# A mixer's 32-partition transpositions replaced by one transposition and ScalarE copies, a PSUM bank lent to side work, and new costs in the build-time scheduler

## The chip, the cores and the metric

The kernel runs on one core of a Trainium2 chip. The metric is the device time of one execution in microseconds. The profile's times are those of one profiled execution; engines are TensorE (PE, with its weight loads PEld), VectorE (DVE), ScalarE (ACT), GpSimd (POOL) and SyncE (SP), whose queue issues nearly all DMAs.

## The reference

One layer of a hybrid decoder for 320 tokens: a prompt of 256 and 8 sample sequences of 8 tokens with their own states. D is 2048, all in fp32. Two recurrent mixers read one input projection:

```
proj = x @ w_in                        # q, k, v, i, f, o of mLSTM; q, f, i, g of HGRN2; two gates
# mLSTM, 4 heads (DK 256, DV 512), stabilised matrix memory
C_new = decay * C + sum_s w_end k_s v_s^T
num   = (q k^T * d) v + w_inter * (q C);  h = num / max(|den|, exp(-m))
branch_a = LayerNorm(h) * ml_norm_g * sigmoid(o)
# HGRN2, 8 heads (DK 128, DV 256)
f = lb + (1 - lb) * sigmoid(hf);  S_t = diag(f_t) S_{t-1} + (1 - f_t) i_t^T;  o_t = S_t^T q_t
branch_b = RMSNorm(o) * hg_norm_g * silu(g)
merged = sigmoid(gate_a) * (branch_a @ w_branch_a) + sigmoid(gate_b) * (branch_b @ w_branch_b)
x1 = LayerNorm(alpha * x + merged @ w_out)
y  = LayerNorm(alpha * x1 + relu(x1 @ w_up)^2 @ w_down)
```

Outputs are y for both groups and the new states: C (4 x 256 x 512, for the prompt and for each of 8 samples), n, m and S.

## The kernel before

**The weight stream.** All weights pass through TensorE as tiles of 128 output columns over 2048 inputs, in the order of tile_list: per mLSTM head four mv, two mk, two mq and two gate tiles (ga); then per HGRN head two gate tiles, hf, hq and two hi; then sixteen o tiles, the rest of the gate tiles (gb), hg and wa in turns, wb, wo, and the FFN's up and dn. A tile is two weight units of 128 x 1024. For each unit SyncE loads the raw weights (tile wr, one of three buffers), ScalarE writes their high part (wh), VectorE the residual (wl, L497), and TensorE does 24 matmuls of 320 columns (L356: high·high, high·low, low·high for eight blocks), 48 a tile, into one PSUM bank. These are the main matmuls. Some wide spare buffers (bb, carved from others later on) serve as wh and wl too.

**Side work.** Everything else, the two mixers above all, runs beside this stream. Each piece is a generator ("chain") that yields operations with an engine and a cost; `Sched` (lines 124 to 243) simulates the five engines while the program is built and emits an operation when its modelled time has come. So the costs and constants of the scheduler don't run on the chip, they set each engine's fixed order. `run_main` emits one triple of main matmuls at a time and calls `pump`, which lets the chains emit what is ready; at most 900 modelled ns of side work go on TensorE between two triples. LAT is added where a step follows one on another engine, SAME where it follows one on the same engine, and PE_LAT is a margin that TensorE's side matmuls must have. act(), dve(), dve_t() (transpositions), pe_f() and pe_r() give costs.

**Banks.** Of eight PSUM banks three belong to the main tiles (mbank) and five to side work (sbank). When a tile is done, its chain `ev_...` reads the bank and gives it back; `take` hands the next tile the bank that is free longest.

**turn.** An mLSTM head's v (1280 elements on each of 128 partitions) and an HGRN head's i (640) must be turned from "channels on partitions" to "tokens on partitions". `turn` does that with 24 VectorE transpositions a head, each from 32 partitions to 32: sixteen at L1156, eight at L1159. VectorE transposes within squares of 32 x 32, so a piece both transposes and moves the squares to other partitions.

**Stacks and states.** `stack` writes high and low parts of the samples' keys side by side (low by VectorE, L987); TensorE transposes them against the identity (L1027 for mLSTM, L1530 for HGRN). For mLSTM's sample states (`m_states`, `m_update`, `m_store`) 64 blocks of 128 x 512 are loaded (C) into one of 14 buffers (cb: six in f, eight in rx), used by matmuls in eight groups of sixteen, updated by VectorE (L1271) and stored (Cs); only after the store has landed is the buffer free for a later block's load. All these DMAs stand on SyncE's queue with the weight loads, the gates that are spilled (gaD), copies of khl and vhl for the prompt's state (kD, vD) and the heads' outputs (hH, hL).

**h_out** normalises an HGRN head's two prompt blocks and transposes each on VectorE (L1631). **ev_o** multiplies an o tile's sigmoid with mLSTM's output and splits it into high and low parts for wa.

The names f_75, f_76 and f_77 in the rows of the order are the SBUF areas f1, f2 and f3; bank_81 to bank_88 are the PSUM banks.

Of the kernel before, what the change touches and what calls it, by code (L numbers as in the profile page):

```python
# [20 lines left out]
TOK = 320  # L21
# [101 lines left out]
LAT = 140.0  # L123
SAME = 100.0
# [19 lines left out]
class Sched:  # L144
# [24 lines left out]
    def step(self, c, now):  # L169
        if c.req is None:  # L170
            try:
                c.req = c.gen.send(c.send)
            except StopIteration:
                c.done = True
                return False
            c.send = None
        kind = c.req[0]
        if kind == "wait":
            for e in c.req[1]:
                if e.t is None:  # L180
                    return False
            c.ready = max([c.ready] + [e.t for e in c.req[1]])
            c.eng = None
        elif kind == "acq":
            pool, n = c.req[1], c.req[2]
            if len(pool.free) < n:
                return False
            pool.free.sort(key=lambda x: x[0])
            got, pool.free = pool.free[:n], pool.free[n:]
            c.ready = max([c.ready] + [x[0] for x in got])  # L190
            c.eng = None
            c.send = got[0][1] if n == 1 else [x[1] for x in got]
# [76 lines left out]
def dve_t(n):  # L269
    return 155.0 + 1.07 * n  # L270
# [43 lines left out]
class Program:  # L314
# [163 lines left out]
    def prep(self, must=False):  # L478
# [103 lines left out]
    def before(self, i, t):  # L582
# [12 lines left out]
        elif kind == "o" and h == 0:  # L595
            s.until(lambda: all(m["end"].t is not None for m in self.mh))
        elif kind == "hg" and h == 0:
            s.until(lambda: all(m["end"].t is not None for m in self.hh))
            self.carve_m()
            self.carve_b()  # L600
            B = self.Part(self.f2)
            for pool in (self.sg, self.sg, self.sr, self.ld, self.ld, self.ld):
                pool.free.append((s.t["pe"], B(320)))
        if kind in ("o", "wa", "hg", "wb"):
            s.spawn(self.fetch(kind, h), 1)
        elif kind == "mk" and h == 0 and c == 0:
            self.load_ev.t = s.t["pe"]
# [312 lines left out]
    def m_S(self, h):  # L920
# [20 lines left out]
        yield ("act", act(128), lambda: self.A(ss[64:128, 0:128], E[64:128, 384:512]))  # L941
# [203 lines left out]
    def turn(self, to, x):  # L1145

        v = self.nc.vector
        n = x.shape[1]
        for a in range(4):
            p = slice(32 * a, 32 * a + 32)  # L1150
            col = lambda y: y.rearrange("p (c a k) -> p a c k", a=4, k=32)[:, a]
            for b in range(4):
# [3 lines left out]
                yield ("dve", dve_t(64 * n), lambda: v.transpose(o, i))  # L1156
            for b in range(2):
                o, i = col(to[64 + 32 * b:96 + 32 * b, 2, :]), x[p, :, NP_ + 32 * b:NP_ + 32 * b + 32]
                yield ("dve", dve_t(32 * n), lambda: v.transpose(o, i))  # L1159
# [143 lines left out]
    def sigmoid(self, p, out, r, free=()):  # L1303
# [9 lines left out]
        yield ("act", act(TOK), lambda: self.A(r, out, AF.Ln, scale=2.0 ** -LN_SH, bias=self.ln_b))  # L1313
        yield ("act", act(TOK), lambda: self.A(r, r, AF.Exp, scale=-1.0, bias=self.exp_b))
# [3 lines left out]
    def ev_hf(self, h, c, b):  # L1318
# [5 lines left out]
        yield ("act", act(TOK), lambda: self.A(u, f, AF.Identity, scale=-1.0, bias=self.one))  # L1324
# [112 lines left out]
    def h_lag(self, b, at):  # L1437
        v = self.nc.vector
        a4 = at[:, 0:TOK].rearrange("p (b r) -> p b r", r=4)
        for d in (0, 2, 1, 3):  # L1440
# [4 lines left out]
            yield ("dve", dve(n, True), lambda: v.copy_predicated(  # L1445
# [4 lines left out]
    def h_put(self, b, at, B):  # L1450
# [3 lines left out]
        elif B >= 32:  # L1454
            for j in range(64 // B):
                for i in range(2):
                    lo, c = 64 * j + B * i, 128 * i + 64 * j
                    yield ("act", act(B, True), lambda: self.A(
# [15 lines left out]
    def h_i(self, h):  # L1474
# [12 lines left out]
        yield ("act", act(256), lambda: self.A(hi, it[64:128, 2, :]))  # L1487
        yield ("dve", dve(256), lambda: v.tensor_tensor(lo, it[64:128, 2, :], hi.bitcast(F32), ALU.subtract))
# [24 lines left out]
    def h_state(self, h):  # L1513
# [18 lines left out]
        for x in range(4):  # L1532
            r = slice(32 * x, 32 * x + 32)
            yield ("act", act(256, True), lambda: self.A(kst[r, x], b[r, 0:256].rearrange("p (g k) -> p g k", g=2)))
# [80 lines left out]
    def h_out(self, h):  # L1615
# [14 lines left out]
        for i in range(2):  # L1630
            yield ("dve", dve_t(256), lambda: v.transpose(on[:, i, :], on[:, i, :]))  # L1631
# [59 lines left out]
    def ev_o(self, j, c, b):  # L1691
# [7 lines left out]
        yield rel(self.ld, x)  # L1699
        yield from self.split(g, self.bah[:, j, :], self.bal[:, j, :])  # L1700
# [388 lines left out]
```

## Time and profile before

| | |
|---|---|
| median of 3 runs | 2305.03 us (2302.9 to 2306.02) |
| the profiled execution | 2302.73 us |
| its span, first to last instruction | 2300.8 us |
| mean granted TensorE clock | 0.999 |
| DMA traffic | 424.94 MB, 185 GB/s |

The profile's page gives busy times, the span in slices, the DMA queues, the chain that ended last, the costliest groups and the DMA issues. A group's row has line, engine, operation, the tiles written and read, the shapes, the count, then busy us and mean ns, then the idle time before its instructions and what ended it. All ScalarE operations pass through one helper and so have line L350, all weight and most side matmuls L356, all SyncE transfers L359. A table by window gives each engine's busy time and count, the granted clock, the DMA engines' mean share and the rate.

### The profile page before, as it was taken

What the parts mean: (1) busy time and instruction counts of PE and PEld (TensorE: products, weight loads), DVE (VectorE), ACT (ScalarE), POOL (GpSimd) and SP (SyncE); (2) the same over time, 40 slices, a digit from 0 to 9 for tenths busy, and PEclk for the clock granted to TensorE, in tenths of its full rate; (3) what the DMA queues carried; (4) which work ended last, traced back from release to release, by engine and by line L of the source; (5) the groups of instructions that cost most, each with busy time, mean ns of one, the idle gap of its engine ahead of it and who ended that gap; (6) DMA issues with size and microseconds to landing.
All of it is one profiled execution on the core that took longest, in us unless ns stands there. A gap on an engine that the chain in (4) does not pass through costs nothing.

```text
span 2300.8 us, 38921 instructions
## 1 busy us (share of the span) xinstructions
PE 2289.6 (100%) x15592; PEld 2246.1 (98%) x15592; DVE 1458.9 (63%) x2634; ACT 1036.6 (45%) x1653; POOL 13.5 (1%) x37
## 2 busy tenths in 40 slices
PE   9999999999999999999999999999999999999998
PEld 9999899999999999999999999999999999999998
DVE  6786786788888886555555767654444444444455
ACT  5443445455555565444433446533433343234334
POOL 0000000000000000000000000000000000000000
PEclk9999999999999999999999999999999999999999
DMA  7667977755565564555545644444444444444475
GB/s 284 211 186 259 295 250 229 259 176 185 191 207 187 166 198 167 180 174 170 176 172 175 214 163 147 147 147 149 154 147 150 152 147 153 149 147 154 149 228 193
DMA packets 214574, 424.94 MB, mean 185 GB/s; under 512 B 83572, under 2 KB 110068, under 8 KB 213368
## 3 DMA queue, kind: packets, MB, share of 16 engines
q1 hardware_dynamic: 209512, 415.97, 53.7%
q0 software_dynamic: 4736, 6.29, 1.0%
q8 instruction: 122, 2.00, 0.3%
q14 instruction: 60, 0.49, 0.1%
q10 hardware_dynamic: 144, 0.20, 0.0%
HBM read 371.48 MB, written 50.90 MB: 184 GB/s over the span
## 4 chain that ended last, share of the span: by engine, by line
PE 69%; DVE 3%; ACT 1%; issue 0%; ACTq 0%; DVEq 0%
PE bank L356 69%; DVE wl L497 1%; ACT wh L350 0%; DVE f L1156 0%; DVE f L1445 0%; ACT f L350 0%; DVE f3m L1973 0%; DVE f3m L1980 0%; ACT f3m L350 0%; DVE f L1159 0%; DVE f L1315 0%; DVE f L1316 0%; DVE f L1631 0%; DVE f L1698 0%; DVE f L1309 0%
## 5 line engine op out<-in xcount | busy, mean ns | idle before, releaser
L356 PE MATMUL bank<-xh,wh 128*128 128x320 f32 (+1 forms) x2504 | 794.6, 318 | 0.0
L356 PE MATMUL bank<-xh,wl 128*128 128x320 f32 (+1 forms) x2504 | 774.8, 310 | 0.0
L356 PE MATMUL bank<-xl,wh 128*128 128x320 f32 (+1 forms) x2504 | 772.2, 309 | 0.0
L497 DVE TENSOR_TENSOR wl<-wr,wh 128x1024 fp32r<-128x1024 f32 x440 | 538.7, 1224 | 361.4 <-ACT wh L350 358.3
L350 ACT ACTIVATE wh<-wr 128x1024 fp32r<-128x1024 f32 x440 | 465.4, 1058 | 524.7 <-PE bank L356 495.6
L356 PEld LDWEIGHTS bank<-xh,wh 128*128 128x128 f32 x2504 | 472.0, 189 | 17.2 <-issue 15.3
L356 PEld LDWEIGHTS bank<-xl,wh 128*128 128x128 f32 x2504 | 471.5, 188 | 3.3
L356 PEld LDWEIGHTS bank<-xh,wl 128*128 128x128 f32 x2504 | 471.8, 189 | 0.2 <-DVE wl L497 0.2
L497 DVE TENSOR_TENSOR bb<-wr,bb 128x1024 fp32r<-128x1024 f32 x162 | 198.5, 1225 | 193.7 <-ACT bb L350 193.5
L350 ACT ACTIVATE bb<-wr 128x1024 fp32r<-128x1024 f32 x162 | 171.6, 1059 | 294.6 <-PE bank L356 277.5
L356 PE MATMUL bank<-ra,wh 128*128 128x320 f32 x1008 | 275.9, 309 | 0.7 <-DVE ra L1672 0.7
L356 PE MATMUL bank<-ra,bb 128*128 128x320 f32 x1096 | 255.2, 309 | 0.0
L356 PE MATMUL bank<-xh,bb 128*128 128x320 f32 (+1 forms) x1136 | 253.8, 309 | 0.0
L356 PE MATMUL bank<-rxb,bb 128*128 128x320 f32 x1088 | 249.0, 309 | 0.0
L356 PEld LDWEIGHTS bank<-xh,bb 128*128 128x128 f32 x1136 | 191.0, 188 | 0.0
L356 PE MATMUL bank<-rxb,wh 128*128 128x320 f32 x608 | 187.5, 308 | 0.0
L356 PE MATMUL bank<-rxb,wl 128*128 128x320 f32 x608 | 187.5, 308 | 0.0
L356 PEld LDWEIGHTS bank<-ra,bb 128*128 128x128 f32 x1096 | 184.9, 187 | 0.0
L356 PEld LDWEIGHTS bank<-rxb,bb 128*128 128x128 f32 x1088 | 184.2, 187 | 0.0
L356 PEld LDWEIGHTS bank<-ra,wh 128*128 128x128 f32 x1008 | 180.9, 187 | 0.9 <-DVE ra L1672 0.9
L356 PE MATMUL bank<-xl,bb 128*128 128x320 f32 (+1 forms) x568 | 175.5, 309 | 0.0
L356 PE MATMUL bank<-bb,wh 128*128 128x320 f32 (+1 forms) x536 | 119.0, 313 | 0.0
(259 smaller groups left out, 2244.4 us busy)
## 6 DMA issues: line engine op xcount, KB each, us to landing
wr<-wt SPq DMA_DIRECT2D x602, 512.0 KB, 3.3
rx<-C SPq DMA_DIRECT2D x34, 256.0 KB, 5.6
Cs<-rx SPq DMA_DIRECT2D x34, 256.0 KB, 4.8
f<-C SPq DMA_DIRECT2D x30, 256.0 KB, 5.5
Cs<-f SPq DMA_DIRECT2D x30, 256.0 KB, 4.1
f<-first SPq DMA_DIRECT2D x6, 704.0 KB, 9.6
vD<-ra SPq DMA_DIRECT2D x4, 1024.0 KB, 5.2
f<-S SPq DMA_DIRECT2D x8, 512.0 KB, 5.0
```

What stands on the lines that cost most here:

```text
L350: return self.nc.scalar.activation(out, in_, func, **kw)
L356: self.nc.tensor.matmul(*a, **kw)
L497: self.V().tensor_tensor(lo, raw, hi.bitcast(F32), ALU.subtract)
```

## The change

Four things. `turn` transposes its source once, in place, on all 128 partitions (VectorE), and then moves the 24 pieces with ScalarE copies; `h_out` transposes two blocks in one instruction. One of the three main banks is lent to side work from the first mk tile to the first hg tile: two main and six side banks in between. `ev_o` waits before its split, for tiles from 7 on, for the last HGRN head's scores (j < 12) or its state (from 12 on). And the scheduler's account: LAT 140 becomes 130; SAME 100 becomes 127 for ScalarE and 113 for VectorE; a step behind TensorE adds 200 (PE_OUT) where it added LAT; transpositions cost 295 + 1.05 n where it was 155 + 1.07 n; operations on part of the partitions cost 122 more (PART); three ScalarE operations with a pointer as bias or scale count it; masked copies get four fixed costs; the weights' two preparations count as 1048 and 1034 elements.

```diff
-LAT = 140.0
-SAME = 100.0
+LAT = 130.0
+SAME = dict(act=127.0, dve=113.0)
+PE_OUT = 200.0
+PART = 122.0
...
-            if c.eng != kind or after:
+            if c.eng == "pe" and kind != "pe" and not after:
+                r += PE_OUT
+            elif c.eng != kind or after:
                 r += LAT
-            elif kind in ("act", "dve"):
-                r += SAME
+            elif kind in SAME:
+                r += SAME[kind]
...
 def dve_t(n):
-    return 155.0 + 1.07 * n
+    return 295.0 + 1.05 * n
...
-        e = s.use("act", max(at, self.raw_at[u]) + LAT, act(1024))
+        e = s.use("act", max(at, self.raw_at[u]) + LAT, act(1048))
...
-        e = s.use("dve", e + LAT, dve(1024))
+        e = s.use("dve", e + LAT, dve(1034))
...
             self.carve_b()
+            self.mbank.free.append(self.sbank.free.pop())
...
         elif kind == "mk" and h == 0 and c == 0:
+            s.until(lambda: self.mbank.free)
+            self.sbank.free.append(self.mbank.free.pop())
...
         n = x.shape[1]
+        t = yield ("dve", dve_t(TOK * n), lambda: v.transpose(x, x))
...
-                yield ("dve", dve_t(64 * n), lambda: v.transpose(o, i))
+                yield ("act", act(64 * n) + PART, lambda: self.A(o, i), (t,))
...
-                yield ("dve", dve_t(32 * n), lambda: v.transpose(o, i))
+                yield ("act", act(32 * n) + PART, lambda: self.A(o, i), (t,))
...
-            yield ("dve", dve(n, True), lambda: v.copy_predicated(
+            yield ("dve", (415.0, 385.0, 320.0, 155.0)[d], lambda: v.copy_predicated(
...
-        yield ("act", act(256), lambda: self.A(hi, it[64:128, 2, :]))
-        yield ("dve", dve(256), lambda: v.tensor_tensor(lo, it[64:128, 2, :], hi.bitcast(F32), ALU.subtract))
+        yield ("act", act(256) + PART, lambda: self.A(hi, it[64:128, 2, :]))
+        yield ("dve", dve(256) + PART, lambda: v.tensor_tensor(lo, it[64:128, 2, :], hi.bitcast(F32), ALU.subtract))
...
-        for i in range(2):
-            yield ("dve", dve_t(256), lambda: v.transpose(on[:, i, :], on[:, i, :]))
+        yield ("dve", dve_t(512), lambda: v.transpose(on[:, 0:2, :], on[:, 0:2, :]))
...
+        if j > 6:
+            yield wait(self.hh[HH - 1]["aT" if j < 12 else "sdone"])
```

The lines left out give PART to four more costs and the pointer to three ScalarE costs. The change adds lines, so in its rows L354 stands for L350, L360 for L356, L363 for L359, L501 for L497 and L994 for L987. What it moves shows in two places.

The first is VectorE in HGRN head 3, before the low part of the samples' stack (L987, then L994) that TensorE's first transposition of this head (L1530 of before) waits for. Before:

```order
L497 TENSOR_TENSOR wl<-wr,wh 128x1024
L1419 TENSOR_TENSOR f_75<-f_75 128x40
L1156 STREAM_TRANSPOSE f_76<-f_75 32x4x32
L1466 COPY_PREDICATED f_75<-lmask,bank_88 128x40x4
L1156 STREAM_TRANSPOSE f_76<-f_75 32x4x32
L1664 TENSOR_SCALAR misc<-misc 128x1
L1056 TENSOR_SCALAR misc<-misc 128x1
L1156 STREAM_TRANSPOSE f_76<-f_75 32x4x32
L987 TENSOR_TENSOR f_76<-f_75,f_76 128x16x8
```

After the change:

```order
L501 TENSOR_TENSOR wl<-wr,wh 128x1024
L1323 SCALAR_TENSOR_TENSOR f_76<-f_76 128x320
L1067 TENSOR_TENSOR misc<-misc 128x1
L1424 TENSOR_TENSOR f_75<-f_75 128x16x8
L1479 COPY_PREDICATED f_75<-lmask,bank_86 128x16x8
L994 TENSOR_TENSOR f_76<-f_75,f_76 128x16x8
```

Three pieces of turn have left the way to the stack. They stand on ScalarE, which in the same head now has:

```order
L354 ACTIVATE wh<-wr 128x1024 x2
L354 ACTIVATE f_76<-f_75 32x4x32 x4
L354 ACTIVATE f_76<-f_75 32x2x32 x2
L354 ACTIVATE f_76<-bank_88,misc 128x256
L354 ACTIVATE f_76<-f_75 32x4x32 x4
L354 ACTIVATE f_76<-f_76 128x320
L354 ACTIVATE f_76<-f_75 32x2x32
L354 ACTIVATE wh<-wr 128x1024
```

Eleven of the 24 pieces stand in a row of side work between two weight copies. The second place is SyncE's queue around the last state load for the first group of mLSTM head 2. Before, from the store that frees the last buffer (the row ahead of vD) to the load into it (the last rx<-C):

```order
L359 DMA Cs<-rx 128x512
L359 DMA vD_114<-ra 128x2048
L359 DMA wr<-wt 128x1024
L359 DMA Cs<-rx 128x512
L359 DMA rx<-C 128x512
L359 DMA Cs<-rx 128x512
L359 DMA rx<-C 128x512
L359 DMA wr<-wt 128x1024
```

After the change, from the load before it:

```order
L363 DMA rx<-C 128x512
L363 DMA Cs<-rx 128x512
L363 DMA kD_110<-ra 32x32x32
L363 DMA Cs<-rx 128x512
L363 DMA kD_110<-ra 32x32x32
L363 DMA wr<-wt 128x1024
L363 DMA hL_200<-f_76 128x4x64
L363 DMA kD_110<-ra 32x32x32
L363 DMA rx<-C 128x512 x2
L363 DMA Cs<-rx 128x512
```

The 1 MB copy vD no longer stands between the store and the load; three of the four copies kD and an output hL stand there instead.

More of the change, by code (lines that the diff above doesn't have):

```diff
@@ L940, in m_S @@
         yield ("act", act(384), lambda: self.A(sh, E[:, 0:384]))
-        yield ("act", act(128), lambda: self.A(ss[64:128, 0:128], E[64:128, 384:512]))
+        yield ("act", act(128) + PART, lambda: self.A(ss[64:128, 0:128], E[64:128, 384:512]))
         yield ("dve", dve(384), lambda: v.tensor_tensor(sl, E[:, 0:384], f(sh), ALU.subtract))
@@ L1312, in sigmoid @@
         yield ("act", act(TOK), lambda: self.A(out, out, AF.Exp))
-        yield ("act", act(TOK), lambda: self.A(r, out, AF.Ln, scale=2.0 ** -LN_SH, bias=self.ln_b))
-        yield ("act", act(TOK), lambda: self.A(r, r, AF.Exp, scale=-1.0, bias=self.exp_b))
+        yield ("act", act(TOK, False, 1), lambda: self.A(r, out, AF.Ln, scale=2.0 ** -LN_SH, bias=self.ln_b))
+        yield ("act", act(TOK, False, 1), lambda: self.A(r, r, AF.Exp, scale=-1.0, bias=self.exp_b))
         yield ("dve", dve(TOK), lambda: v.scalar_tensor_tensor(out, out, 1.0, r, ALU.add, ALU.mult))
@@ L1323, in ev_hf @@
         yield ("dve", dve(TOK, mode=2), lambda: v.tensor_scalar(f, u, l1, lb, ALU.mult, ALU.add))
-        yield ("act", act(TOK), lambda: self.A(u, f, AF.Identity, scale=-1.0, bias=self.one))
+        yield ("act", act(TOK, False, 1), lambda: self.A(u, f, AF.Identity, scale=-1.0, bias=self.one))
         yield post(m["fd"])
@@ L1457, in h_put @@
                     lo, c = 64 * j + B * i, 128 * i + 64 * j
-                    yield ("act", act(B, True), lambda: self.A(
+                    yield ("act", act(B, True) + PART, lambda: self.A(
                         at[64 * j:64 * j + B, c + B:c + 2 * B], b[lo:lo + B, c // 2:c // 2 + B]))
@@ L1533, in h_state @@
             r = slice(32 * x, 32 * x + 32)
-            yield ("act", act(256, True), lambda: self.A(kst[r, x], b[r, 0:256].rearrange("p (g k) -> p g k", g=2)))
+            yield ("act", act(256, True) + PART, lambda: self.A(kst[r, x], b[r, 0:256].rearrange("p (g k) -> p g k", g=2)))
         yield rel(self.sbank, b)
```

## Prediction

> **What bounds the kernel now.** I read the busy shares first, then the busy time by stage, then the waits of TensorE, then single places on the timeline. The page's first row, and four rows of the table by stage (window, length, then busy time and count of PE, PEld, DVE, ACT, POOL, granted clock, DMA share, GB/s):
>
> ```profile
> PE 2289.6 (100%) x15592; PEld 2246.1 (98%) x15592; DVE 1458.9 (63%) x2634; ACT 1036.6 (45%) x1653; POOL 13.5 (1%) x37
> 180.00:406.00 226.00, 225.78 (x1520) 209.27 (x1519) 172.20 (x340) 102.30 (x169) 0.00 (x0) 1.00 0.79 255
> 300.00:350.00 50.00, 50.00 (x343) 44.49 (x342) 45.37 (x96) 22.02 (x36) 0.00 (x0) 1.00 0.92 291
> 420.00:860.00 440.00, 437.37 (x3055) 426.68 (x3054) 370.89 (x961) 248.81 (x534) 4.74 (x13) 1.00 0.60 192
> 860.00:2277.00 1417.00, 1416.34 (x9648) 1415.62 (x9647) 759.07 (x999) 579.59 (x764) 5.90 (x8) 1.00 0.47 162
> ```
>
> TensorE sets the end. From 860 to 2277 us it does 9648 matmuls in 1417 us, one every 147 ns at granted clock 1.00, and that stretch keeps its order on TensorE; nothing is to be had there. A gain can only come from 93 to 860 us, where the two recurrent mixers run beside the weights. There TensorE seems full too, but a busy row hides part of a wait: a matmul is booked for 0.31 us while the next starts 0.147 us after it. VectorE is the crowded helper (172.20 of 226 us in the mLSTM stage, 370.89 of 440, 84%, in the HGRN stage); ScalarE has room (102.30 of 226, 248.81 of 440, 57%). The waits of TensorE say who is late (engine, line, waited for: us in total, times, longest):
>
> ```profile
> PE bank L1530 <- DVE f L987: 1.5, 3, 0.7
> PE bank L356 <- DVE rh L1488: 1.1, 2, 0.6
> ...
> PE bank L1212 <- DVE f L1049: 0.7, 1, 0.7
> PE bank L356 <- DVE ra L1672: 0.7, 1, 0.7
> ```
>
> The three rows on L987, L1488 and L1049 are VectorE work that the mixers need. Their six waits make 3.3 us, and each hides up to 0.16 us in the booking (0.31 − 0.147), so at most 4.3 us. The row L1672 is one wait after 860 us, where the order stays. One of the six on the timeline (start, duration, engine, line):
>
> ```profile
> 603.36 0.30 PE L356 MATMUL bank<-xh,wl 128*128 128x320 f32 x1
> 603.65 0.31 DVE L1156 STREAM_TRANSPOSE f<-f 32x128 f32<-32x128 f32 x1
> ...
> 604.33 0.33 PE L1530 MATMUL bank<-cst,f 128*128 128x128 f32 x1 [0.67 <-DVE f L987]
> ```
>
> TensorE stands with a transposition (L1530) at the head of its queue, with the weight stream behind it, until VectorE has subtracted (L987); VectorE does one of turn's pieces (L1156) first. The two TensorE starts are 0.97 us apart instead of about 0.15.
>
> **Turn, and what moves with it.** What leaves VectorE and what stands for it (groups: count, busy us, mean ns), then ScalarE copies of a similar size:
>
> ```profile
> L1156 DVE STREAM_TRANSPOSE f<-f 32x128 f32<-32x128 f32 (+1 forms) x160 | 56.9, 356 | 3.8
> ...
> L1159 DVE STREAM_TRANSPOSE f<-f 32x64 f32<-32x64 f32 (+1 forms) x80 | 21.2, 265 | 1.9
> ...
> L1090 DVE STREAM_TRANSPOSE f<-f 128x512 f32<-128x512 f32 x8 | 5.7, 709 | 0.2
> ```
> ```profile
> L350 ACT ACTIVATE f3h<-f 128x128 f32<-128x128 f32 x12 | 3.7, 306 | 3.8 <-DVE f L1416 3.8
> ...
> L350 ACT ACTIVATE rh<-f 64x256 fp32r<-64x256 f32 x8 | 3.3, 415 | 2.1 <-DVE f L1159 1.9
> ```
>
> Twelve heads call turn, 24 pieces each: 192 pieces of L1156 at 0.356 and 96 of L1159 at 0.265 are 93.8 us of VectorE. In their place stands one transposition a head, of 640 elements in an HGRN head and 1280 in an mLSTM head; in proportion to the row of 512 elements (0.709) at most 0.89 and 1.77, 8 × 0.89 + 4 × 1.77 = 14.2 us. In h_out two transpositions of 256 become one of 512, which can't take longer than the two. So VectorE loses about 80 us. ScalarE gains 64 copies of 256 elements at 0.415 and 224 smaller ones at no more than 0.306: at most 95 us, nearly all of it in the two stages, where it had 124 us free (226 − 102) in the shown two thirds of the one and 191 (440 − 249) in the other.
>
> The end only feels this where VectorE was late. Setting VectorE's work between two residuals (L497), with the trace's durations, against TensorE's place, in the order before and in the changed one, I find 33 side steps of TensorE that stand no later than their VectorE step, the worst 1.9 us short, and after the change ten, none more than 0.25 short. So I take most of the 4.3 us: **−3.5 us**. The bounds are 0 (each wait replaced by another) and −4.3. The cover for ScalarE's copies is that its free time lies between the weight copies (1.06 us each); a copy late by one piece costs TensorE at most one 0.415. Of ScalarE's steps ahead of a TensorE step only one or two come out short, by about 0.5: **+0.3 us**, 0 to +1.5.
>
> TensorE's own work is the same in kind, but side steps now fall together more often: in the order 381 interruptions of the weight stream become 373. The pair of starts around an interruption costs more than the matmuls in it; the eight that vanish, all of fp32 matmuls, I estimate at about 0.125 each: **−1.0 us**, 0 to −1.0.
>
> **The accounting.** The new constants issue nothing. They move work: mLSTM's state updates stand earlier. TensorE runs them in eight groups of sixteen matmuls, before at main matmuls 549, 663, 1041, 1353, 1536, 1839, 1980 and 2346, now at 570, 684, 975, 1185, 1419, 1593, 1854 and 1980. Each group needs eight blocks of state loaded into one of 14 buffers that an earlier update has to free: update (VectorE), store, landing, load, landing. The two groups that waited most, with one between that did not, then the store and the load of the last one's freeing chain, from the timeline, and the median landing time of the loads in the busiest stretch, 300 to 350 us (count, KB each, us):
>
> ```profile
> 180.07 1.06 PE L356 MATMUL bank<-f 128*32 128x512 f32 x8
> ...
> 182.72 0.41 PE L356 MATMUL bank<-xh,wh 128*128 128x320 f32 x1
> ...
> 232.36 1.06 PE L356 MATMUL bank<-rx,f 128*32 128x512 f32 x8
> ...
> 234.22 0.42 PE L356 MATMUL bank<-xh,wh 128*128 128x320 f32 x1
> ...
> 266.04 0.62 PE L356 MATMUL bank<-f 128*32 128x512 f32 x2
> ...
> 268.18 1.05 PE L356 MATMUL bank<-rx,f 128*32 128x512 f32 x2 [0.22 <-DMA rx<-C]
> 269.15 0.41 PE L356 MATMUL bank<-xh,wh 128*128 128x320 f32 x1
> ```
> ```profile
> 257.34 0.38 SPq L359 DMA_DIRECT2D Cs<-rx  x1
> 262.34 0.42 SPq L359 DMA_DIRECT2D rx<-C  x1
> ```
> ```profile
> rx<-C SPq DMA_DIRECT2D x8, 256.0 KB, 5.5
> ```
>
> From the first matmul of a group to the next weight matmul the undisturbed group takes 1.86 us, the others 2.65 and 3.11: 0.79 + 1.25 = 2.0 us are lost now, though the waits of TensorE name 0.2 (the bracket). In the chain of the group at 266 the store was issued at 257.34, the load at 262.34, and TensorE went on at 268.18. In the order, the update that frees its last buffer stood 2.1 weight units (24 matmuls, 3.5 us) before the group and now stands 1.5 before it; for the group at 180 (main matmul 1041), 2.8 became 2.1; for those at 1353, 1839 and 2346, 1.7, 1.7 and 2.0 became 1.8, 1.6 and 1.9; at 1980 it is over 3.5 in both. So two groups lose 0.6 and 0.7 units, 4.6 us, if the chain takes as long as before. But SyncE's queue has less between store and load of the first of them, and the chain shortens where it waits less for earlier entries. Bounds −2.0 (no load late any more) and +4.6; I take a value a little under the middle: **+1.0 us**.
>
> [...]
>
> **The sixth side bank** is a main bank lent from the first mk tile to the first hg tile. With two, a tile can start when the tile before the last is evacuated, so the evacuation has one tile, 48 × 0.147 = 7.1 us. The slowest of before, from the last matmul of an hf tile to VectorE's end:
>
> ```profile
> 539.65 0.31 PE L356 MATMUL bank<-xh,wl 128*128 128x320 f32 x1
> ...
> 542.60 0.48 DVE L1309 TENSOR_SCALAR f<-bank 128x320 f32<-128x320 f32 x1
> ```
>
> That is 3.4 us, half of what there is: **0**. If VectorE or ScalarE fell 3.7 us further behind, each tile would cost TensorE the rest. The Trainium skill, "Perfetto Trace Analysis", section "Optimizing Tensor Performance", wants independent groups to rotate through different banks so that evacuation overlaps, which speaks against lending one; the 3.4 us say two are enough here. The new wait in ev_o holds only the split of the o tiles from 7 on, until the last HGRN head is through. The first reader of all of them, the first wa tile, stands behind the first hg tile, and that tile waits for the last head anyway; nothing else is queued behind it but its own buffers. The tail's order changes in two small VectorE copies and one store: 0 ± 0.3.
>
> **Sum.** −3.5 + 0.3 − 1.0 + 1.0 + 0 = −3.2 us. The profiled execution took 2302.7 us (span 2300.8); it becomes 2299.5. The median of the runs before, 2305.0, lies 2.3 us above that execution, so the time I predict is **2301.8 us**.
>
> **Rivals.** (1) *Every wait goes, the loads' too*: −4.3 − 1.0 − 2.0 = −7.3, 2297.7 us. For it: VectorE is freed by 80 us, so updates and stores come sooner in time than their place in the order says; against it: SyncE's queue and the 5.5 us landing don't get shorter. (2) *The gain is given back at the loads*: −3.5 + 0.3 − 1.0 + 4.6 = +0.4, 2305.4 us. For it: the two shortened leads; against it: a shorter queue. (3) *Slower: the squeezed state traffic saturates the transfers*, in the mLSTM stage. Between the second and the eighth group 48 loads and 56 stores of 256 KB, 27.3 MB, are moved in 1683 main matmuls. One takes 0.174 us with the side work (1041 to 1536 between 180.07 and 266.04), so that is 293 us and 93 GB/s; in 1296 main matmuls it becomes 121, and the stage's 255 GB/s about 283. If landing then grows by 2.3 us, five groups (all but the one with the long lead) wait that much more: +11.5, in sum +8.3, 2313.3 us. It decides from 0.64 us more per group on (3.2 / 5). For it: two groups wait already at 0.79 DMA share. Against it: 300 to 350 us ran at 291 GB/s and 0.92 with TensorE at 50.00 of 50 us and loads landing after 5.5. (4) *The rearrangement doesn't free VectorE where it counts*, or two banks do stall tiles: ten tiles late by 0.5 us would undo all, about 2307.
>
> **How the numbers follow.** Forecast 0.45 (own range 2299 to 2304), rival 1 0.20, rival 2 0.17, rival 3 0.15, rival 4 0.03. The terms' lower ends together give −7.3 and 0.3 of the tail, 2297.4; the runs of before spread by −2.1 and +1.0 about their median, and with a part of that the range starts at 2296.8. Above, it takes in rival 2 with ScalarE's full 1.5 and a late VectorE wait or two: 2308.0; rival 3 stays outside. Faster by over 0.2% (4.6 us, about what a measurement of this kernel tells from no change) means below 2300.4: rival 1 and four tenths of the forecast, 0.38. Slower by as much, above 2309.6: rivals 3, 4 and the edge of 2, 0.20. Within: 0.42.
>
> **What would show it.** Right: the rows for L987, L1488 and L1049 gone or under 1 us; VectorE near 1379 us, ScalarE near 1130; the row for L1672 still 0.7; 860 to 2277 us unchanged in length. The groups of state matmuls tell the fourth term: first start to next weight matmul 1.9 us each for rival 1, 4 to 6 us in the groups at 975 and 1419 main matmuls for rival 2, over 4 us in five of them with landing at 8 us for rival 3. A gap on TensorE at a tile's first matmul with an evacuation behind it would show rival 4. The forecast fails if new waits on ScalarE's pieces exceed 1.5 us, or if the stretch after 860 us is not the same.

## The result, and the profile after

The changed kernel takes 2297.77 us (median of 13 runs, 2296.03 to 2299.87), the kernel before 2303.94 (13 runs on the same chips, 2302.07 to 2306.02). The ratio is 0.9974, 95% interval [0.9967, 0.9982]: 6.2 us less, with an interval of 4 to 8 us. The forecast was 3.2 us less.

The profiled execution took 2297.64 us, 5.1 below the one of before. Where that went can be read from the starts of the main matmuls. Let "the stretch" be the time from the 301st main matmul (at 54 us, before the mixers) to the 5535th (some 940 us; behind it both kernels run TensorE alike). It took 888.97 us before and 885.24 after: 3.73 less. Another 0.8 was saved before the stretch, but its start lies between 53.7 and 54.8 us in the fourteen profiles of this study, whatever was changed; that is an execution's own spread. The remaining 0.5 lies at the end and outside the span. The busy row of the page, and the table by stage (as before: window, length, busy time and count of PE, PEld, DVE, ACT, POOL, clock, DMA share, GB/s):

```profile
PE 2286.6 (100%) x15592; PEld 2245.6 (98%) x15592; DVE 1369.2 (60%) x2350; ACT 1125.5 (49%) x1941; POOL 13.4 (1%) x37
```
```profile
180.00:406.00 226.00, 224.49 (x1519) 208.42 (x1518) 157.03 (x311) 120.16 (x220) 2.47 (x7) 1.00 0.82 257
420.00:860.00 440.00, 439.85 (x3081) 430.87 (x3080) 314.22 (x757) 301.21 (x722) 2.20 (x6) 1.00 0.59 188
860.00:2277.00 1417.00, 1416.34 (x9636) 1414.64 (x9635) 758.83 (x1001) 580.87 (x769) 5.89 (x8) 1.00 0.50 163
300.00:350.00 50.00, 50.00 (x345) 47.35 (x344) 35.16 (x69) 31.17 (x60) 0.00 (x0) 1.00 0.94 299
```

VectorE fell by 89.7 us (about 80 were forecast) and ScalarE rose by 88.9 (at most 95). In the HGRN stage the two now stand level (314 and 301 of 440 us) and TensorE's busy time went up to 439.85 of 440. From 860 to 2277 us nothing changed. All waits of TensorE that the trace names are now these:

```profile
PE bank L360 <- DMA rx<-C: 1.8, 2, 1.5
PE bank L360 <- POOL ones L647: 1.0, 1, 1.0
PE bank L360 <- DVE ra L1679: 0.7, 1, 0.7
```

The three rows on VectorE work of the mixers are gone. The row of L1672 is unchanged (the line is L1679 now), and the state loads have become the largest. They are late for the third and the fifth group, on TensorE's timeline:

```profile
168.16 1.06 PE L360 MATMUL bank<-f 128*32 128x512 f32 x8
169.04 1.03 PE L360 MATMUL bank<-rx,f 128*32 128x512 f32 x6
170.39 1.04 PE L360 MATMUL bank<-rx,f 128*32 128x512 f32 x2 [0.31 <-DMA rx<-C]
171.37 0.41 PE L360 MATMUL bank<-xh,wh 128*128 128x320 f32 x1
...
247.72 0.62 PE L360 MATMUL bank<-f 128*32 128x512 f32 x2
...
251.15 1.05 PE L360 MATMUL bank<-rx,f 128*32 128x512 f32 x2 [1.51 <-DMA rx<-C]
252.13 0.41 PE L360 MATMUL bank<-xh,wh 128*128 128x320 f32 x1
```

From first start to next weight matmul they take 3.21 and 4.41 us where the undisturbed group takes 1.86. SyncE's queue shows why for the second of them, from the store that frees the last buffer to the load into it:

```profile
239.02 0.38 SPq L363 DMA_DIRECT2D Cs<-rx  x1
239.45 0.42 SPq L363 DMA_DIRECT2D kD<-ra  x1
239.97 0.89 SPq L363 DMA_DIRECT2D Cs<-rx  x1
240.90 1.02 SPq L363 DMA_DIRECT2D kD<-ra  x1
241.97 2.91 SPq L363 DMA_DIRECT2D wr<-wt  x1
244.98 0.38 SPq L363 DMA_DIRECT2D hL<-f  x1
245.40 0.50 SPq L363 DMA_DIRECT2D kD<-ra  x1
246.00 0.82 SPq L363 DMA_DIRECT2D rx<-C  x1
```

The load goes out 7.0 us after the store (before: 257.34 to 262.34, 5.0), behind a weight load that itself held the queue for 2.9 us, and 1.7 us before its group begins; TensorE goes on 5.2 us after the load was issued.

### The profile page after: what moved, and what is told of

It is laid out like the page before. It is cut to its first block, busy times and chain, and to the rows that moved or that the text cites. A ratio compares the mean times of both kernels' runs of the same rounds, so it can differ in the third digit from the quotient of the medians.

```text
span 2295.9 us, 38951 instructions
## 1 busy us (share of the span) xinstructions
PE 2286.6 (100%) x15592; PEld 2245.6 (98%) x15592; DVE 1369.2 (60%) x2350; ACT 1125.5 (49%) x1941; POOL 13.4 (1%) x37
## 4 chain that ended last, share of the span: by engine, by line
PE 97%; ACT 1%; DVE 1%; DMA 1%; issue 0%; SPq 0%; ACTq 0%; POOL 0%; DVEq 0%; POOLq 0%
PE bank L360 97%; DMA rx<-C 1%; ACT f L354 1%; ACT wh L354 0%; DVE f3m L1982 0%; DVE f3m L1989 0%; ACT f3m L354 0%; PE bank L1538 0%; PE bank L1034 0%; PE bank L1648 0%; SPq L363 0%; PE bank L1220 0%; DVE wl L501 0%; ACT oC L354 0%; ACT xh L354 0%
## 5 line engine op out<-in xcount | busy, mean ns | idle before, releaser
L501 DVE TENSOR_TENSOR wl<-wr,wh 128x1024 fp32r<-128x1024 f32 x440 | 538.9, 1225 | 441.8 <-ACT wh L354 437.0
L360 PE MATMUL bank<-xh,wh 128*128 128x320 f32 (+1 forms) x2504 | 793.5, 317 | 0.0
L360 PE MATMUL bank<-xh,wl 128*128 128x320 f32 (+1 forms) x2504 | 774.6, 310 | 0.0
L360 PE MATMUL bank<-xl,wh 128*128 128x320 f32 (+1 forms) x2504 | 771.8, 309 | 0.0
L354 ACT ACTIVATE wh<-wr 128x1024 fp32r<-128x1024 f32 x440 | 465.6, 1058 | 495.2 <-PE bank L360 477.1
L360 PEld LDWEIGHTS bank<-xh,wh 128*128 128x128 f32 x2504 | 471.6, 189 | 17.0 <-issue 14.7
L360 PEld LDWEIGHTS bank<-xl,wh 128*128 128x128 f32 x2504 | 471.2, 188 | 3.3
L360 PEld LDWEIGHTS bank<-xh,wl 128*128 128x128 f32 x2504 | 471.5, 188 | 0.2 <-DVE wl L501 0.2
L354 ACT ACTIVATE bb<-wr 128x1024 fp32r<-128x1024 f32 x162 | 171.6, 1059 | 295.3 <-PE bank L360 277.1
L501 DVE TENSOR_TENSOR bb<-wr,bb 128x1024 fp32r<-128x1024 f32 x162 | 198.5, 1225 | 194.3 <-ACT bb L354 194.1
L360 PE MATMUL bank<-ra,wh 128*128 128x320 f32 x1008 | 275.9, 309 | 0.7 <-DVE ra L1679 0.7
L360 PE MATMUL bank<-ra,bb 128*128 128x320 f32 x1096 | 255.2, 309 | 0.0
L360 PE MATMUL bank<-xh,bb 128*128 128x320 f32 (+1 forms) x1136 | 253.8, 309 | 0.0
L360 PE MATMUL bank<-rxb,bb 128*128 128x320 f32 x1088 | 249.0, 308 | 0.0
L360 PEld LDWEIGHTS bank<-xh,bb 128*128 128x128 f32 x1136 | 191.0, 188 | 0.0
L360 PE MATMUL bank<-rxb,wh 128*128 128x320 f32 x608 | 187.6, 308 | 0.0
L360 PE MATMUL bank<-rxb,wl 128*128 128x320 f32 x608 | 187.5, 308 | 0.0
L360 PEld LDWEIGHTS bank<-ra,bb 128*128 128x128 f32 x1096 | 184.8, 187 | 0.0
L360 PEld LDWEIGHTS bank<-rxb,bb 128*128 128x128 f32 x1088 | 184.3, 187 | 0.0
L360 PEld LDWEIGHTS bank<-ra,wh 128*128 128x128 f32 x1008 | 180.9, 187 | 0.9 <-DVE ra L1679 0.9
L360 PE MATMUL bank<-xl,bb 128*128 128x320 f32 (+1 forms) x568 | 175.5, 309 | 0.0
L354 ACT ACTIVATE f<-f 128x320 f32<-128x320 f32 (+5 forms) x413 | 152.8, 370 | 24.8 <-DVE f L1317 9.3
```

The lines of the kernel that those rows point to most:

```text
L354: return self.nc.scalar.activation(out, in_, func, **kw)
L360: self.nc.tensor.matmul(*a, **kw)
L501: self.V().tensor_tensor(lo, raw, hi.bitcast(F32), ALU.subtract)
```

## The experiments

All twelve other kernels are measured against the kernel before on the same chip. The last three columns are from one profile each: the stretch as above; what TensorE lost at groups of side matmuls (the time between the two main matmuls around a group, less what the same group takes where nothing is late in any of the fourteen profiles), once for late VectorE and ScalarE work and once for late state loads. Composed groups that occur in few profiles are in the stretch only. The profile of e6_turn_bank is of the slowest of its four runs, 4.8 us above their median.

| kernel | median us | ratio to before [95%] | stretch us | VectorE and ScalarE late | loads late |
|---|---|---|---|---|---|
| before | 2303.94 | | 888.97 | 5.9 | 2.5 |
| changed | 2297.77 | 0.9974 [0.9967, 0.9982] | 885.24 | 0.7 | 4.1 |
| e1_turn | 2326.34 | 1.0098 [1.0085, 1.0112] | 913.08 | 26.6 | 3.6 |
| e2_costs | 2306.05 | 1.0011 [1.0002, 1.002] | 891.25 | 6.6 | 2.5 |
| e3_bank | 2303.65 | 0.9998 [0.999, 1.0007] | 890.83 | 7.7 | 2.2 |
| e4_no_bank | 2300.99 | 0.999 [0.9981, 0.9999] | 886.60 | 1.1 | 0.2 |
| e5_old_turn | 2295.44 | 0.9964 [0.995, 0.9977] | 882.41 | 0.9 | 1.1 |
| e6_turn_bank | 2332.46 | 1.0126 [1.0112, 1.0139] | 922.88 | 29.5 | 8.2 |
| e7_lead15 | 2296.54 | 0.9967 [0.9954, 0.9979] | 883.33 | 0.5 | 2.5 |
| e8_lead30 | 2294.32 | 0.9957 [0.9945, 0.997] | 880.71 | 0.4 | 0.2 |
| e9_turn_part | 2298.30 | 0.9974 [0.9964, 0.9984] | 883.98 | 1.7 | 1.2 |
| e10_lat | 2302.52 | 0.9994 [0.9985, 1.0003] | 890.61 | 6.6 | 3.3 |
| e11_cost | 2304.01 | 1.0001 [0.9992, 1.0009] | 889.81 | 3.7 | 3.5 |
| e12_old_lead | 2299.27 | 0.9979 [0.997, 0.9988] | 885.38 | 2.4 | 0.1 |

**The parts alone.** Theory A was the forecast's: turn's pieces leave VectorE, so what TensorE waits for comes in time. Its rivals were that the corrected account does it (B) or the lent bank (C).

e1_turn, the new turn and h_out's single transposition in the kernel before:

```diff
+        t = yield ("dve", dve_t(TOK * n), lambda: v.transpose(x, x))
...
-                yield ("dve", dve_t(64 * n), lambda: v.transpose(o, i))
+                yield ("act", act(64 * n), lambda: self.A(o, i), (t,))
...
-                yield ("dve", dve_t(32 * n), lambda: v.transpose(o, i))
+                yield ("act", act(32 * n), lambda: self.A(o, i), (t,))
```

> The kernel before with the new turn and the merged transposition of h_out alone; old costs and constants, five side banks, no wait in ev_o. Theory A (freeing VectorE is the gain): TensorE's waits for VectorE (rows of the stack's low part, of rh and of the sample numerator's normalisation: 3.3 us in the kernel before) fall under 1 us, and the time falls by 4 to 6 us, to about 2298 to 2300. Theory B (the corrected costs are the gain, since they put TensorE's steps behind what is late): the waits stay over 2 us, 2303 to 2305. Theory C (the sixth side bank is the gain): no change. The loads of state: groups of state matmuls stand within 50 main matmuls of where they stood, so the three late groups should lose about 2.5 us as before.

Every theory missed: 22.7 us slower. VectorE had the forecast's relief (1369.6 us busy), but TensorE now waits for ScalarE. The first waits of TensorE in this kernel, then ScalarE and TensorE on its timeline at 694 us:

```profile
PE bank L356 <- ACT f L350: 11.6, 7, 2.4
PE bank L356 <- ACT f3h L350: 2.8, 2, 1.6
PE bank L356 <- DVE rh L1489: 2.7, 2, 2.0
```
```profile
695.36 0.56 ACT L350 ACTIVATE f<-f,misc 128x320 f32<-128x320 f32 x1
695.95 0.52 ACT L350 ACTIVATE f<-f 32x64 f32<-32x64 f32 x2
696.49 0.28 ACT L350 ACTIVATE f<-bank 128x128 f32<-128x128 f32 x1
696.78 0.56 ACT L350 ACTIVATE f<-f,misc 128x320 f32<-128x320 f32 x1
697.25 0.24 ACT L350 ACTIVATE f<-f 128x64 f32<-128x64 f32 x1
697.39 1.04 ACT L350 ACTIVATE wh<-wr 128x1024 fp32r<-128x1024 f32 x1
```
```profile
694.81 0.31 PE L356 MATMUL bank<-xh,wl 128*128 128x320 f32 x1
697.54 0.70 PE L356 MATMUL bank<-f 128*128 128x256 f32 x2 [2.42 <-ACT f L350]
```

ScalarE runs without a pause, and TensorE's next side step needs what stands at the end of that run (697.25). The groups of the copies in this kernel give the reason:

```profile
L350 ACT ACTIVATE f<-f 32x128 f32<-32x128 f32 x128 | 39.4, 308 | 10.2 <-DVE f L1149 6.9 <-DVE f3h L1420 1.7
L350 ACT ACTIVATE f<-f 32x256 f32<-32x256 f32 x64 | 26.6, 415 | 6.8 <-DVE f L1149 6.0
L350 ACT ACTIVATE f<-f 32x64 f32<-32x64 f32 x48 | 12.2, 253 | 0.6
```

The old account says act(128) = (112 + 128) / 1.2 = 200 ns, 307 for 256 and 147 for 64. The copies take 106 to 108 ns more each: 24 × 0.107 = 2.6 us a head that the scheduler doesn't know of. In the last three heads TensorE was held once each for about that long, 2.7 us over the group's own price at 694.8, 2.8 at 747.3 and 2.7 at 801.4.

The lengths of the records don't say why these copies in particular are counted too low: a 128x128 copy lasts 306 ns and is counted at 200 as well. The starts do. In the rows of 694 us, the weight copy starts 0.14 us after a 128x64 copy that lasts 0.24, which is what the account says of it (147 ns); behind two 32x64 copies the next operation starts only after 0.54 us, 0.27 each. Over this trace, a weight copy right behind a 128x128 copy starts 201 ns after its start (median of 5), behind one of turn's 32x128 copies 333 ns (median of 12). So the operation behind one of turn's copies doesn't overlap with it, and each costs some 0.12 to 0.13 us more of ScalarE's time than the account says.

e9_turn_part puts this to the test by mending that one cost (PART of the changed kernel, here on turn's copies alone):

```diff
-                yield ("act", act(64 * n), lambda: self.A(o, i), (t,))
+                yield ("act", act(64 * n) + 122.0, lambda: self.A(o, i), (t,))
```

> The kernel before with the new turn and the merged transposition of h_out, and one cost corrected: the 24 ScalarE copies count 122 more each. Nothing else of the account, five side banks. Theory D (the new turn alone took 2326 us because ScalarE's copies last longer than the account says, so that all that follows on ScalarE is late on the chip): TensorE's waits for ScalarE, 14.4 us there, fall under 3 us and the time to 2301 to 2308. Rival (ScalarE is simply too full, or turn's pieces stand in the way of the weights' high parts wherever they are): the waits stay over 8 us, over 2315.

2298.30 us, better than the theory's range: no wait for ScalarE is left, and those for VectorE are nearly gone too. The first four rows of its waits:

```profile
PE bank L356 <- POOL ones L640: 1.0, 1, 1.0
PE bank L356 <- DVE ra L1672: 0.7, 1, 0.7
PE bank L356 <- DVE rh L1489: 0.5, 2, 0.2
PE bank L1027 <- DVE f L987: 0.2, 1, 0.2
```

So the new turn with its own cost told truly is as fast as the whole change (both 0.9974), with five side banks and with all other old constants. Theory D is shown. Theory A stands, with this condition and one reservation: with the longer cost the heads' side work also ends later, behind main matmul 5184 instead of 4932, so this run alone doesn't separate a freer VectorE from steps that stand later. In the changed kernel the waits are gone and side work ends at 4908, no later than before.

e2_costs is the account alone: old turn, five side banks. It also lacks the wait in ev_o, so that late o tiles are split over memory the last head still uses, and part of its output is wrong.

> The changed kernel's costs and constants alone: turn on VectorE in 24 pieces, five side banks, no wait in ev_o. Theory A: VectorE is as full as before (1459 us busy), so some of the 3.3 us of waits stay; 2302 to 2304. Theory B: the waits are gone, as in the changed kernel, 2298 to 2300. Theory C: 2304. The state groups stand later or as before (at 873 instead of 663, last at 2220 instead of 2346 main matmuls), so the loads should cost no more than 2.5 us.

The waits inside the heads were gone (of its 6.6 us, 5.7 are one place), so B had that right; but the time was a little worse. This is the one place among TensorE's waits:

```profile
PE bank L1645 <- ACT f L354: 5.3, 1, 5.3
```

It stands behind 5376 main matmuls, before the first of hg: there the main stream waits until all heads are through, and with the new costs the heads' side work ended only there, where it ended at main matmul 4932 in the kernel before.

e3_bank lends the bank in the kernel before:

```diff
+            s.until(lambda: self.mbank.free)
+            self.sbank.free.append(self.mbank.free.pop())
...
+            self.mbank.free.append(self.sbank.free.pop())
```

> The kernel before with the lent bank alone. An update of states takes four side banks at once, so with six instead of five it leaves two for the rest, and groups four to eight move from main matmul 1353, 1536, 1839, 1980, 2346 to 1185, 1395, 1617, 1881, 2100. Theory A and B: VectorE's waits stay at 3 to 4 us and the loads of state come late more often: 4 us instead of 2.5; 2304 to 2306. Theory C: under 2301. If two main banks stall tiles, a wait of TensorE for a tile's evacuation shows and the time is over 2307.

No change (0.9998), as A and B said, except that the loads didn't come late more often (2.2 us). Two main banks stalled nothing here: none of its waits is one for a tile's evacuation. e4_no_bank takes the same three lines out of the changed kernel:

> The changed kernel with three main and five side banks throughout. The state groups stand at 1095, 1425, 1563, 2010, 2136, 2511 instead of 975, 1185, 1419, 1593, 1854, 1980. Theories A and B: waits for VectorE stay under 1 us, the loads of state cost 0 to 2.5 us instead of 4.0; 2295.5 to 2298. Theory C: the gain is gone, 2302 to 2305.

Both forecasts were half right. The loads lose only 0.2 us and the waits in the heads stay away, yet the median is 3.2 us above the changed kernel's and the stretch 1.4. TensorE's timeline shows where it went; the first and last rows are main matmuls of neighbouring tiles:

```profile
850.16 0.31 PE L360 MATMUL bank<-xh,wl 128*128 128x320 f32 x1
850.40 1.07 PE L360 MATMUL bank<-f3h 128*32 128x256 f32 x16
...
858.08 0.64 PE L360 MATMUL bank<-xh,wh 128*128 128x320 f32 x1 [1.88 <-DVE f L1314]
```

An o tile can't start for 7.8 us, in which only the last head's side work runs. The wait named is for the evacuation (L1314) of the bank it needs; by the code, o tiles wait in ev_o for that head and hold their buffers, and so the next evacuation comes late. Side work ends at main matmul 5268 here, at 4908 in the changed kernel. An update of states takes four side banks at once; with five only one is left for all else. So the sixth bank is worth something under the new costs and turn, 1.4 us by the stretch and 3.2 by the medians (the two intervals just touch), though the loads lose 3.9 us more with it; under the old ones it is worth nothing.

**The account with the old turn.** e5_old_turn is the changed kernel with turn and h_out as before.

```diff
-        t = yield ("dve", dve_t(TOK * n), lambda: v.transpose(x, x))
...
-                yield ("act", act(64 * n) + PART, lambda: self.A(o, i), (t,))
+                yield ("dve", dve_t(64 * n), lambda: v.transpose(o, i))
```

> The changed kernel with turn in 24 VectorE pieces and h_out's two transpositions as before; new costs, the lent bank and the wait in ev_o stay. Theory A (freeing VectorE is the gain): waits of TensorE for VectorE come back, 2 to 4 us, and the time is 2301 to 2304. Theory B (the costs are the gain): the waits stay under 1 us and the time is 2297 to 2299, as in the changed kernel. ScalarE falls back to about 1037 us and VectorE rises to about 1459 in both.

Theory B's number, and better: 2295.44 us with VectorE at 1456.2 us. Its waits of TensorE, complete:

```profile
PE bank L360 <- POOL ones L647: 1.0, 1, 1.0
PE bank L360 <- DVE ra L1679: 0.7, 1, 0.7
PE bank L360 <- DVE ra L971: 0.5, 1, 0.5
```

A full VectorE is no harm if the order allows for its work: TensorE's steps then stand later, and side work ends at main matmul 5196 instead of 4932. For turn's pieces the new account is also the nearer one. In the trace of before, a 32x128 piece starts 31 ns behind the end of the operation before it, where operations on 128 partitions mostly start 82 ns before that end, and the next starts 333 ns after it (medians): an estimated 0.45 us with what the neighbour loses, counted at 292 ns before and at 429 now. For transpositions on 128 partitions it is a margin: 640 elements count 967 ns, and in the changed kernel the next operation starts after 762.

So each of the two, the turn with its true cost (e9) and the account with bank and wait in ev_o (e5), removes the waits without the other; together they can't remove them twice. Of e5's three parts, the account alone (e2) stalled before hg; whether the bank or the wait in ev_o prevents that was not tested. e6_turn_bank completes the square, the new turn and the bank with the old account:

> The kernel before with the new turn and the lent bank, old costs. The state groups stand at 558, 663, 1020, 1158, 1374, 1497, 1851, 1956 main matmuls, closest of all. Theory A: waits for VectorE under 1 us, loads of state late by 4 us or more as in the changed kernel; 2297 to 2300. Theory B: waits for VectorE of 2 to 4 us on top, 2301 to 2304.

As with e1, all expectations fell with the copies' cost: 28.6 us slower, 29.5 us of late VectorE and ScalarE work. The bank doesn't help it; state work is packed closer still and the loads lose 8.2 us.

e10_lat and e11_cost halve the account, each with old turn, bank and the wait in ev_o: the constants between steps (LAT, SAME, PE_OUT) in the one, the operations' costs in the other.

> The old turn with the lent bank and the wait in ev_o, and of the account only the three constants for the time between steps (LAT, SAME, PE_OUT); all operation costs as before. If these constants cured the waits of TensorE for VectorE and ScalarE (5.1 us in the rows of the kernel before with the bank alone: 3.3 us, without the rows for ones and the layer norm), they fall under 1 us and the time is 2295 to 2298. If the operations' costs did it, 2 us or more stay and the time is 2301 to 2304.

> The complement: old turn, lent bank, wait in ev_o, and of the account only the operations' costs (transpositions 140 ns longer, operations on part of the partitions, pointers, masked copies, the weights' preparation); LAT 140 and SAME 100 as before. If the operations' costs cured the waits: under 1 us, 2295 to 2298; if the constants did: 2 us or more, 2301 to 2304. Both halves could also be needed: then both this and its complement lie between, at 2298 to 2301.

Neither half gains, and neither lies between 2298 and 2301 us, as was expected if both were needed. With the constants alone sixteen places of late VectorE and ScalarE work remain. With the costs alone almost nothing is left in the heads, but one place at 90 us has a new wait, and the loads lose 3.5 us:

```profile
PE bank L357 <- DVE ra L968: 2.7, 1, 2.7
```

A second place isn't in the table's columns: at 850 us an o tile's first matmul comes 3.2 us after the main matmul before it, with a wait of 0.8 us for its bank. The costs cure the waits and both halves together keep new ones away; which single cost does most is open.

**The loads.** e7_lead15 and e8_lead30 are the changed kernel with one line changed, so that TensorE's state group is placed later, as if the loads landed 1500 or 3000 ns later than the scheduler believes:

```diff
-            m["parts"][n].t = t
+            m["parts"][n].t = t + 3000.0
```

> The changed kernel, with a state block counted as there 1500 ns later than the scheduler's account of its load says. If the late groups (3.4 and 4.5 us from first matmul to next weight matmul instead of 1.95) wait because the load is believed too early, they lose 1.0 to 2.5 us less: 4.0 becomes about 2 us, and the time is 2295 to 2297. If they wait because the transfers are saturated (a later group makes its successors' loads later too), the sum stays near 4 us.

> The same with 3000 ns. Believed too early: all groups at 1.95 us, 4.0 us gone, 2293.5 to 2295.5 us. Saturated: no gain over the changed kernel, 2297 to 2299.

The loads' loss fell from 4.1 to 2.5 and 0.2 us and the time to 2296.54 and 2294.32: believed too early, not saturated. The fifth group in e8_lead30, undisturbed:

```profile
242.04 0.62 PE L360 MATMUL bank<-f 128*32 128x512 f32 x2
...
242.50 1.46 PE L360 MATMUL bank<-rx,f 128*32 128x512 f32 x10
243.89 0.41 PE L360 MATMUL bank<-xh,wh 128*128 128x320 f32 x1
```

This is the fastest version found: 0.9957 [0.9945, 0.997] of the kernel before, against 0.9974 [0.9967, 0.9982] for the change; the intervals touch, the stretches (880.71 and 885.24) agree with the medians.

e12_old_lead gives e5's kernel the same 3000 ns.

> The best found so far, put together: the account, the lent bank and the wait in ev_o with turn on VectorE as before, and a state block counted as there 3000 ns later. With the old turn the loads of state cost 1.1 us, so at most that can go: 2294 to 2296, no more than 1 us from the changed kernel with the same 3000 ns (2294.3). If the new turn has a worth of its own once the loads are not late, this one stays over 2295.5.

It missed, at 2299.27. The loads are early (0.1 us lost), but side work that was already late, ending at main matmul 5196, now holds up an o tile at 846 us, with a wait for its bank:

```profile
849.71 0.41 PE L360 MATMUL bank<-xh,wh 128*128 128x320 f32 x1 [1.39 <-DVE f L1316]
```

So the new turn does have a worth of its own once loads are not late: e8, which differs from this kernel in turn and h_out alone, has a stretch shorter by 4.7 us and side work that ends at 4908. That the shorter side work is what leaves room to place steps later is argued: in e5 side work ends at 5196 too, and no o tile is held up.

## Why the prediction was right, and where not

**The bound** held: TensorE full after 860 us, all change between 93 and 860.

**The waits for VectorE**, −3.5 with a bound of −4.3. The mechanism was right, and the new turn is enough by itself once its copies are priced (e9); the size was too small: 5.9 us became 0.7, so −5.2. The step that failed is "their six waits make 3.3 us, and each hides up to 0.16 us". The waits' view names a wait only where TensorE is booked idle. Measured from start to start, ten places were late by more than 0.15 us, 5.5 us together: the six named ones by 0.2 us more than named on average, and four short ones (512.4, 513.3, 348.4 and 804.1 us) not named at all. The six alone make 4.6 us, already over the bound. The bound should have been taken from the starts.

**ScalarE's copies**, +0.3: right in the changed kernel, where no wait for ScalarE is named. But the cover was put down to ScalarE's free time between weight copies. e1 has the same free time and loses 22.7 us; the cover is the cost that the account gives the copies. That their price was right (0.306 and 0.415 us, taken from copies on 128 and 64 partitions) was luck in part: the records are equally long, but the operation behind a 128x128 copy starts after 201 ns.

**The interruptions**, −1.0: 365 became 357 in the stretch, as counted, but the stretch leaves only −3.73 + 5.2 − 1.6 = −0.1 for them, so the eight that went cost next to nothing, not 0.125 each, a figure for which the prediction shows no rows. The starts say why: from the main start ahead of a group to the third behind it, a lone 128x128 transposition costs the stream at least 0.105 us, a lone 128x256 matmul (rh,ra) 0.111 and both in one group 0.228. An interruption has no price beside its matmuls; these least prices add up to 109.7 us in the stretch before and 109.8 after. The term should have been 0.

**The loads**, +1.0: 2.5 became 4.1, so +1.6, in the two groups that were named and inside the bounds (the prediction had 2.0 for before; it left out 0.45 at 406 us). The cause was given wrongly: the prediction puts the earlier places of the state updates down to the new constants. For groups four to eight it is the bank. e3 has the old account and these groups at 1185, 1395, 1617, 1881 and 2100; e4 has the new account without the bank and they stand at 1425, 1563, 2010, 2136 and 2511. It was overlooked that an update asks for four side banks of five. The third group, one of the two late ones, is moved by no part alone: it stands at 1041 in e3 and e5, at 1095 in e4 and at 975 only in the changed kernel. Nor does an earlier place make a load late by itself: e3's fifth group, at 1395, takes its least time.

**The bank**, 0: right that two main banks stall no tile in the changed kernel and in e3, wrong that it is worth nothing; e4 shows 1.4 to 3.2 us. What it buys (side work that ends in time) wasn't a term of the sum. The sum was not spoilt by it, since its terms were read from the changed order, which had the bank's effect in it.

**Rivals.** The saturated transfers didn't come: 300 to 350 us ran at 299 GB/s and 0.94 with TensorE busy for 50.00 of 50 us, and e8 at still more. Rival 2's sign, 4 to 6 us in the two late groups, came half: 3.21 and 4.41. Rival 1 has the number that was measured (2297.7), but not for its reason: it lets the loads' waits go, and they grew.

The Trainium skill ("Perfetto Trace Analysis", "Optimizing Tensor Performance") wants independent groups to rotate through different banks so that evacuation overlaps. Two main banks still rotate, and lending the third cost nothing in e3 (2303.65 us against 2303.59). In e11 and e12, also with two, one o tile waits for its bank (0.8 and 1.4 us), and in e4 one does so with three (1.9 us).

**The sum.** The forecast of −3.2 came close to the stretch (−3.7) with some luck: the waits gave 2.0 us more than their two terms, the interruptions 0.9 less and the loads cost 0.6 more, and these errors nearly cancel. Of what the medians have beyond the stretch (−6.2), 1.2 us is that the profiled execution of before was below its median (2302.73 and 2303.94); the rest is the spread of starts and the end.

## What to carry to other kernels

When a build-time order feeds a saturated engine, an operation's cost in the planner is as much a part of a change as the operation: moving 90 us of work to a less busy engine lost 23 us with a cost 35% too low and gained 6 with the right one. Measure from start to start, the waits of a pipelined engine (the named ones showed 3.3 of 5.5 us) and the price of an operation (two copies with records of 0.31 us took 0.20 and 0.33). Test the parts of a combined change alone and left out: here the turn with its price, and the account with bank and wait, each gave the whole gain, and the bank was worth nothing or 1 to 3 us depending on the others.

## What was not expected of the hardware

A ScalarE copy between 32 partitions has a record as long as one on 128 (308 ns for 32x128 in e1, 306 for 128x128 in the kernel before), but it costs more: a weight copy starts 333 ns after the one and 201 after the other in e1 (medians). VectorE shows the same with turn's old pieces: 31 ns behind the operation before them, where two operations on 128 partitions mostly overlap by 82 ns. That fits the 89.7 us by which VectorE's busy time fell, where the records of the replaced instructions add up to 80.2 less. Whether it is the number of partitions or the move from some partitions to others that ends the overlap, no run separates.

One VectorE transposition on 128 partitions takes 842 ns for 640 elements, where the 24 pieces of such a head took 303 ns (sixteen) and 238 (eight) each; the 356 and 265 ns of the rows shown before are means over two sizes. It leaves the moving to other partitions to the copies:

```profile
L1156 DVE STREAM_TRANSPOSE f<-f x10: 836/842/1504, 44.3 to 770.7; 128x640 f32<-128x640 f32 x6, 128x1280 f32<-128x1280 f32 x4
L1156 DVE STREAM_TRANSPOSE f3h<-f3h x2: 834/835/836, 520.8 to 720.4; 128x640 f32<-128x640 f32 x2
```

(Minimum, median and maximum in ns, first and last start, forms; the changed kernel.) The row of 512 elements taken in proportion had given 0.89 us and 1.77; measured were 0.84 and 1.50.
